# Half of each modulation row handed from VectorE to ScalarE and GpSimd during the SwiGLU stages

## The chip, the cores and the metric

The kernel runs on one core of a Trainium2 chip. The metric is the device time of one execution in microseconds (us). The engines are named as in the profile: PE is TensorE (matmul), PEld its weight load, DVE VectorE, ACT ScalarE, POOL GpSimd, SP SyncE, which here only issues DMAs. A "q" behind an engine's name (SPq, ACTq) means its instruction queue.

## What is computed

A two-layer decoder trunk on 256 tokens of width 1024 in float32. Each layer is a half-step SwiGLU feed-forward (width 2816), a token mixer (block-sparse attention, "MoBA", in the first layer; latent attention, "MLA", in the second), and another half-step SwiGLU. Each of these six sub-layers starts with an RMS norm that is modulated by a shift and a scale, and ends in a gate; all three vectors come from a conditioning vector `c`:

```
mods = silu(c) @ ada_w[layer] + ada_b[layer]          # 1024 x 9216 per layer
sh1, sc1, g1, sh2, sc2, g2, sh3, sc3, g3 = split(mods, 9)
h = rms_norm(x, g) * (1 + sc) + sh
x = x + 0.5 * gate * ((silu(h @ w_gate) * (h @ w_up)) @ w_down)
```

The shared keys and values of MLA have a shift and a scale of their own (`kv_ada_w`, 1024 x 2048). So there are 20 modulation vectors of 1024 numbers. The first two are made at the start in code of their own; the other 18 are what this change is about.

## The kernel before, in words

**Matmuls.** A float32 product is done as three products of split operands (`mm3`, lines 393 to 397): each operand is split into a rounded part `hi` and a rest `lo`. For a weight tile, `split` (lines 174 to 179) lets ACT copy 1024 columns of `raw` into `hi`, and DVE subtract to get `lo = raw - hi`. Hidden activations are split in the same way (`gh`/`gl`, `hh`/`hl`). All of these are recorded under lines 196 and 198, inside the helper `in_turn`, so the profile tells them apart by tile names.

**Loading weights.** `wload` (360 to 380) issues a DMA of up to 1 MB from SP's queue into one of three `raw` buffers and splits it. `hi` and `lo` have eight buffers of 1024 columns each, and `nextw` keeps one load ahead (`LOOK = 1`). A `raw` buffer is free again when DVE has made its `lo`.

**Modulation vectors.** `ada_vec` (201 to 235) makes one vector of 1024 numbers. For each of eight blocks of 128 rows of the weight (`k` from 0 to 7) it loads a 128 x 1024 block into one of three `adaw` buffers from SP's queue (line 209), and DVE adds it, times a column of `silu(c)`, to the 128 x 1024 accumulator `acc` (line 211, one `scalar_tensor_tensor`). I call one such step a row. The bias row is preloaded into the tile `bz`, which stands in for `acc` in the first step. After the eighth row the accumulator is summed over partitions on PE, by transposes and a reduction (lines 222 and 257) for shift and scale, or by a matmul with ones (230 and 231) for gates. There is one `acc` buffer. 

**The order of the work.** Rows are woven into the stages by a clock that adds up estimated PE time (`pe`, `ada_pace`, `ada_until`): in each SwiGLU stage (`ffn`, 506 to 589) they are spread evenly over `FFN_PACE` = 172 us, and what is left is emitted before the next norm (line 584). Stage one gets five vectors (40 rows), MoBA one (8 rows), the second SwiGLU six (48 rows), the third five (40), the last one (8). `tc.issue_after` (in `behind`) keeps rows behind the hand-ordered start-up. Beyond that a scheduler places instructions in the engines' queues; each engine runs its queue strictly in order, and waits on semaphores where an operand or a buffer is not ready.

**The stages in time** (from the trace): start to 47 us; first SwiGLU to about 236; MoBA to about 369; second SwiGLU to about 561; third to about 757; MLA to about 870; last SwiGLU to the end. During the first SwiGLU the kernel also builds MoBA's bias table: DVE makes one-hot tiles `oh`, PE multiplies them, ACT copies them to `bt`, POOL masks two of them (`affine_select`, line 785), and SP writes them to memory (line 788).

**Other lines named below.** POOL raises to a power for every inverse standard deviation: `rstd` (429 for the norms, 992 for MLA's latents) and `hr` (703 for heads). MLA's latent norm is `lat_norm_T` (985 to 1004): ACT squares (`junk`, 988), DVE adds epsilon (`var`, 990), POOL takes the power, DVE scales (`ly`, 994). `head_rstd` (695 to 704) begins with ACT's `sq` (698).

Of the kernel before, what the change touches and what calls it, by code (L numbers as in the profile page):

```python
# [14 lines left out]
AF = mybir.ActivationFunctionType  # L15
ALU = mybir.AluOpType
# [5 lines left out]
D = 1024  # L22
# [65 lines left out]
def trunk(ctx: ExitStack, tc: tile.TileContext, a: dict, out: bass.AP):  # L88
    nc = tc.nc
# [14 lines left out]
    def nm(s):  # L104
        uid[0] += 1
        return f"{s}_{uid[0]}"
# [9 lines left out]
    def later(us, fn):  # L116
        uid[0] += 1
        bisect.insort(pend, (clock[0] + us, uid[0], fn))
# [11 lines left out]
    def pe(us):  # L130
        clock[0] += us
        if busy[0]:
            return
        while pend and pend[0][0] <= clock[0]:
            run_next()
        while pace[0] and clock[0] >= pace[1]:
            pace[1] += pace[0]
            ada(1)
# [15 lines left out]
    bz = cp.tile([P, D], F32, name="bz")  # L154
# [7 lines left out]
    cact = cp.tile([P, KD], F32, name="cact")  # L162
# [11 lines left out]
    def split(src, n):  # L174
        hi = splitp.tile([P, n], F32R, tag="hi", name=nm("hi"))
        lo = splitp.tile([P, n], F32R, tag="lo", name=nm("lo"))
        in_turn(nc.scalar.activation, hi, src, AF.Copy, on="a")
        in_turn(nc.vector.tensor_tensor, lo, src, hi.bitcast(F32), op=ALU.subtract, on="v")
        return hi, lo
# [4 lines left out]
    @contextmanager  # L184
    def behind(*engines):

        with ExitStack() as es:
            for e in engines:
                if e in chain:
                    es.enter_context(tc.issue_after(chain[e].ins))  # L190
            yield

    def in_turn(fn, *args, on="p", **kw):
# [4 lines left out]
            chain[on] = fn(*args, **kw)  # L198
        return chain[on]

    def ada_vec(w, b, col, finish, rows):


        acc = adap.tile([P, D], F32, tag="acc", name=nm("acc"), bufs=1)
        nc.scalar.dma_start(bz[0:1, :], b[col:col + D].rearrange("(o n) -> o n", o=1))
        for k in range(KD):
            wt = adap.tile([P, D], F32, tag="adaw", name=nm("adaw"))
            with behind("s"):
                nc.sync.dma_start(wt, w[k * P:(k + 1) * P, col:col + D])
            with behind("v"):  # L210
                nc.vector.scalar_tensor_tensor(acc, wt, cact[:, k:k + 1], bz if k == 0 else acc,  # L211
                                               op0=ALU.mult, op1=ALU.add)
            if k < KD - 1:
                yield
        if rows:
            ahi, alo = split(acc, D)

        def col_sums():
            for hh in range(2):
                pt = ps_tr.tile([P, 512], F32, tag="tr", name=nm("adaps"))  # L220
                for j in range(4):
                    nc.tensor.transpose(kslice(pt, j), kslice(acc, 4 * hh + j), ident)  # L222
                pe(0.44)
                finish(hh, pt)

        def sums():
            for hh in range(2):
                pt = ps_tr.tile([P, 512], F32, tag="tr", name=nm("adaps"))
                sl = slice(hh * 512, (hh + 1) * 512)
                nc.tensor.matmul(pt, ones_r, ahi[:, sl], start=True, stop=False)  # L230
                nc.tensor.matmul(pt, ones_r, alo[:, sl], start=False, stop=True)
                pe(0.44)
                finish(hh, pt)
        later(3.0, sums if rows else col_sums)
        yield
# [58 lines left out]
    def ada(n):  # L294
        for _ in range(n):
            if next(ada_it, "end") != "end":
                ada_done[0] += 1
# [7 lines left out]
    def ada_until(vectors):  # L305
        pace[0] = None
        while ada_done[0] < vectors * KD:
            ada(1)
# [90 lines left out]
    def mm_tile():  # L399
        return ps_mm.tile([P, 512], F32, tag="mm", name=nm("mm"))  # L400
# [101 lines left out]
    def kslice(tile_, k):  # L502
        return tile_[:, k * P:(k + 1) * P]


    def ffn(layer, idx, h, after, ada_to, start=None):

        last = (layer, idx) == (1, 1)
        with ExitStack() as st:
            gp = st.enter_context(tc.tile_pool(name=nm("gp"), bufs=1))  # L510
            gT = {}
            accs = start() if start else {t: [] for t in range(NT)}
            ada_pace(ada_to, 90.0 if last else FFN_PACE)
            parts = [] if start else [[], []]
            for t in range(NT):
                for i, pl in enumerate(parts):
                    ps = mm_tile()
                    for k in range(KD):
                        if len(pl) <= k:
                            pl += nextw()  # L520
                        mm3(ps, *hk(h[t], k), *pl[k], start=k == 0, stop=k == KD - 1)
                    accs[t].append(ps)
                acc = accs.pop(t)
                g = gp.tile([P, FB], F32, tag="g", name=nm("g"), bufs=2)
                nc.scalar.activation(g, acc[0], AF.Silu)
                nc.vector.tensor_tensor(g, acc[1], g, op=ALU.mult)

                def fin(t=t, g=g):
                    pt = tr_tile()
                    for j in range(FB // P):  # L530
                        nc.tensor.transpose(kslice(pt, j), kslice(g, j), ident)
                    pe(FB // P * 0.11)
                    gh, gl = [gp.tile([P, FB], F32R, tag=f"{nme}_{t}", name=nm(nme)) for nme in ("gh", "gl")]
                    split_evac(gh, gl, pt)
                    for j in range(FB // P):
                        gT[j, t] = (kslice(gh, j), kslice(gl, j))
                later(G_WAIT, fin)
            gq = gp
            for f0 in range(FB, F, S):
                if f0 == SIDE_TO * S:  # L540
                    while start and next(side[0], "end") != "end":
                        bias_step()
                    gq = st.enter_context(tc.tile_pool(name=nm("gp"), bufs=1))
                if start and f0 == ROPE_AT * S:
                    with behind("v", "a", "g"):
                        rope_tables()
                        mla_consts()
                parts = [[], []]
                for f in range(f0 // P, (f0 + S) // P):
                    ps = mm_tile().rearrange("p (i t q) -> p i t q", i=2, q=P)  # L550
                    for i, pl in enumerate(parts):
                        for k in range(KD):
                            if len(pl) <= k:
                                pl += nextw()
                            mm3(ps[:, i], *[w[:, f * P - f0:(f + 1) * P - f0] for w in pl[k]],
                                *hk_both(h, k), start=k == 0, stop=k == KD - 1)
                            if start and k in HOOKS and f0 < SIDE_TO * S:
                                bias_step()
                    g = gp.tile([P, NT, P], F32, tag="gT", name=nm("g"), bufs=2)
                    nc.scalar.activation(g, ps[:, 0], AF.Silu)  # L560
                    nc.vector.tensor_tensor(g, ps[:, 1], g, op=ALU.mult)  # L561
                    gh, gl = [gq.tile([P, NT, P], F32R, tag=f"{nme}{f}", name=nm(nme)) for nme in ("gh", "gl")]
                    split_evac(gh, gl, g)
                    for t in range(NT):
                        gT[f, t] = gh[:, t, :], gl[:, t, :]
            for half in range(2):
                acc = [mm_tile() for _ in range(NT)]
                wl = []

                def mms(t, k):  # L570
                    until(lambda: (k, t) in gT)
                    mm3(acc[t], *gT[k, t], *wl[k], start=k == 0, stop=k == KF - 1)

                lag = LAG if half == 1 else 0
                for k in range(KF):
                    if len(wl) <= k:
                        wl += nextw()
                    mms(0, k)
                    if k - lag >= 0:
                        mms(1, k - lag)  # L580
                gate = mod((layer, 2 * idx), "g")
                resid(0, half, acc[0], gate, last)
                if half == 1:
                    ada_until(ada_to)
                    after(0)
                    for k in range(KF - lag, KF):
                        mms(1, k)
                resid(1, half, acc[1], gate, last)
            after(1)
# [695 lines left out]
```

## Time and profile before

| | |
|---|---|
| median of 3 runs | 1062.43 us (1061.85 to 1064.68) |
| the profiled execution's own time | 1067.16 us |
| its span, first to last instruction | 1065.4 us |
| mean granted clock of TensorE | 0.998 |
| PE busy in the span | 1020.8 us (96%) |
| ACT busy | 578.6 us (54%) |
| data moved by DMA | 260.65 MB, mean 245 GB/s |

The profile gives, for one execution, the busy time of each engine, groups of instructions by line and shape, what each wait ended on, and a timeline. "Busy" of PE is drawn from modelled ends of pipelined matmuls, so gaps of a fraction of a microsecond inside a dense run do not show. In the tables by stretch, the figure behind an engine is its busy time inside that stretch, with the number of instructions in brackets.

### The profile page before, as it was taken

How to read it: one execution, taken by the hardware profiler on the slowest of the kernel's cores; microseconds unless marked ns; L12 is line 12 of the kernel's file. 1: busy time of each engine (PE TensorE's matmuls, PEld its weight loads, DVE VectorE, ACT ScalarE, POOL GpSimd, SP SyncE). 2: the span in 40 equal slices, each digit the busy share in tenths (PEclk: the TensorE clock that was granted, in tenths of full speed). 3: DMA queues.
4: the chain of work that ended last, by engine and by line, in shares of the span. 5: the costliest groups of instructions: out<-in, count | busy, mean ns of one | idle time of the engine just before them, and what ended most of it. 6: DMA issues, size and time to landing. Idle time of an engine off the chain costs nothing.

```text
span 1065.4 us, 17278 instructions
## 1 busy us (share of the span) xinstructions
PE 1020.8 (96%) x6663; PEld 899.3 (84%) x6663; DVE 810.9 (76%) x1244; ACT 578.6 (54%) x1048; POOL 70.1 (7%) x119
## 2 busy tenths in 40 slices
PE   4999999998999999999999999999988899999998
PEld 2499999886778789999887999988766778999986
DVE  5999977886875789889688888867778758755642
ACT  4364545357675765545348544533868777545531
POOL 4001000002121000000000000000043200000000
PEclk9999999999999999999999999999999999999999
DMA  9999987996845479989897997986354337665450
GB/s 311 322 304 287 376 288 278 335 318 206 310 162 170 139 236 345 337 293 332 295 313 227 328 329 251 318 303 205 117 162 142 119 119 236 223 204 187 161 177 20
DMA packets 166934, 260.65 MB, mean 245 GB/s; under 512 B 8030, under 2 KB 110214, under 8 KB 166852
## 3 DMA queue, kind: packets, MB, share of 16 engines
q1 hardware_dynamic: 164496, 254.70, 70.3%
q0 software_dynamic: 976, 3.37, 1.0%
q10 hardware_dynamic: 1380, 1.49, 0.5%
q8 instruction: 52, 0.85, 0.3%
q14 instruction: 30, 0.25, 0.1%
HBM read 255.33 MB, written 4.19 MB: 244 GB/s over the span
## 4 chain that ended last, share of the span: by engine, by line
PE 77%; DVE 10%; ACT 4%; DMA 4%; POOL 3%; issue 3%; SPq 0%; DVEq 0%; ACTq 0%; POOLq 0%
PE mm L394 23%; PE mm L396 23%; PE mm L395 23%; DVE lo L196 3%; POOL hr L703 3%; DMA adaw<-in_ada_w_dram 2%; PE mm L198 2%; ACT hi L196 1%; DVE oh L722 1%; PE adaps L222 1%; PE at L666 1%; PE at L611 1%; DVE acc L211 1%; DMA raw<-in_ffn_w_gate_dram 1%; ACT y L196 1%
## 5 line engine op out<-in xcount | busy, mean ns | idle before, releaser
L196 DVE TENSOR_TENSOR lo<-raw,hi 128x1024 fp32r<-128x1024 f32 (+2 forms) x316 | 374.3, 1199 | 80.2 <-ACT hi L196 79.3
L196 ACT ACTIVATE hi<-raw 128x1024 fp32r<-128x1024 f32 (+2 forms) x316 | 324.1, 1040 | 171.5 <-PE mm L396 103.6
L394 PE MATMUL mm<-hh,hi 128*128 128x256 f32 x1152 | 328.6, 285 | 0.0
L396 PE MATMUL mm<-hh,lo 128*128 128x256 f32 x1152 | 326.7, 284 | 0.5 <-DVE lo L196 0.5
L395 PE MATMUL mm<-hl,hi 128*128 128x256 f32 x1152 | 326.5, 283 | 0.0
L395 PEld LDWEIGHTS mm<-hl,hi 128*128 128x128 f32 x1152 | 221.7, 192 | 0.6 <-issue 0.2
L396 PEld LDWEIGHTS mm<-hh,lo 128*128 128x128 f32 x1152 | 221.6, 192 | 0.7 <-DVE lo L196 0.7
L394 PEld LDWEIGHTS mm<-hh,hi 128*128 128x128 f32 x1152 | 221.7, 192 | 0.6 <-issue 0.2
L211 DVE SCALAR_TENSOR_TENSOR acc<-adaw,cact,acc 128x1024 f32<-128x1024 f32 x126 | 162.8, 1292 | 20.6 <-DMA adaw<-in_ada_w_dram 16.2
L394 PE MATMUL mm<-hi,gh 128*128 128x512 f32 x352 | 138.0, 392 | 0.0
L395 PE MATMUL mm<-lo,gh 128*128 128x512 f32 x352 | 137.0, 389 | 0.0
L396 PE MATMUL mm<-hi,gl 128*128 128x512 f32 x352 | 137.0, 389 | 0.0
L394 PE MATMUL mm<-hi,hh 128*128 128x512 f32 (+1 forms) x240 | 96.7, 404 | 5.0 <-ACT hh L196 5.0
L396 PE MATMUL mm<-hi,hl 128*128 128x512 f32 (+1 forms) x240 | 94.0, 392 | 1.5 <-DVE hl L196 1.4
L395 PE MATMUL mm<-lo,hh 128*128 128x512 f32 (+1 forms) x240 | 93.4, 390 | 0.0
L560 ACT ACTIVATE g<-mm 128x256 f32<-128x256 f32 x72 | 27.3, 379 | 94.5 <-PE mm L396 94.5
L396 PEld LDWEIGHTS mm<-hi,gl 128*128 128x128 f32 x352 | 66.1, 188 | 13.8
L394 PEld LDWEIGHTS mm<-hi,gh 128*128 128x128 f32 x352 | 66.1, 188 | 13.2
L395 PEld LDWEIGHTS mm<-lo,gh 128*128 128x128 f32 x352 | 66.1, 188 | 13.1
L196 ACT ACTIVATE gh<-g 128x256 fp32r<-128x256 f32 x72 | 29.9, 416 | 69.6 <-DVE g L561 69.6
L394 PEld LDWEIGHTS mm<-hi,hh 128*128 128x128 f32 x240 | 45.1, 188 | 16.1 <-ACT hh L196 7.8
L396 PEld LDWEIGHTS mm<-hi,hl 128*128 128x128 f32 x240 | 45.1, 188 | 13.2 <-DVE hl L196 4.5
(222 smaller groups left out, 1114.8 us busy)
## 6 DMA issues: line engine op xcount, KB each, us to landing
adaw<-in_ada_w_dram SPq DMA_DIRECT2D x144, 512.0 KB, 6.8
raw<-in_ffn_w_gate_dram SPq DMA_DIRECT2D x42, 1024.0 KB, 7.3
raw<-in_ffn_w_up_dram SPq DMA_DIRECT2D x42, 1024.0 KB, 6.9
raw<-in_ffn_w_down_dram SPq DMA_DIRECT2D x40, 1024.0 KB, 6.6
raw<-in_moba_w_qkv_dram SPq DMA_DIRECT2D x16, 512.0 KB, 5.0
adaw<-in_kv_ada_w_dram SPq DMA_DIRECT2D x16, 512.0 KB, 5.6
raw<-in_ffn_w_down_dram SPq DMA_DIRECT2D x8, 512.0 KB, 3.6
raw<-in_moba_w_qkv_dram SPq DMA_DIRECT2D x4, 1024.0 KB
```

What stands on the lines that cost most here:

```text
L196: return fn(*args, **kw)
L198: chain[on] = fn(*args, **kw)
L211: nc.vector.scalar_tensor_tensor(acc, wt, cact[:, k:k + 1], bz if k == 0 else acc, op0=ALU.mult, op1=ALU.add)
L222: nc.tensor.transpose(kslice(pt, j), kslice(acc, 4 * hh + j), ident)
L394: nc.tensor.matmul(ps, lh, rh, start=start, stop=False)
L395: nc.tensor.matmul(ps, lh, rl, start=False, stop=False)
L396: nc.tensor.matmul(ps, ll, rh, start=False, stop=stop)
L560: nc.scalar.activation(g, ps[:, 0], AF.Silu)
L611: nc.tensor.matmul(ps3[:, i, :], qTs(e, t), kTs(e, nk), start=bias is not None, stop=bias is not None or i == len(es) - 1)
L666: nc.tensor.matmul(po[i * DH:(i + 1) * DH, pr, t, :], vs(e, kb), pT[t, e, kb], start=kb == 0, stop=kb == t)
L703: nc.gpsimd.tensor_tensor(r, v2, mhalf[:, :nh], op=ALU.pow)
L722: return fn(*args, **kw)
```

## The change

In the SwiGLU stages DVE does only the left 512 columns of each row (`acc[:, :n]`). For the right 512 columns ACT multiplies the loaded block by the column of `silu(c)` in place, and POOL adds it to the accumulator. A flag, set when a SwiGLU stage is entered and cleared just before the next norm, says where this holds: 136 of the 144 rows; the eight rows of the MoBA stage stay whole on DVE.

```diff
+    shared = [False]
+
     def ada_vec(w, b, col, finish, rows):
...
             with behind("s"):
                 nc.sync.dma_start(wt, w[k * P:(k + 1) * P, col:col + D])
+            old = bz if k == 0 else acc
+            n = D // 2 if shared[0] else D
             with behind("v"):
-                nc.vector.scalar_tensor_tensor(acc, wt, cact[:, k:k + 1], bz if k == 0 else acc,
+                nc.vector.scalar_tensor_tensor(acc[:, :n], wt[:, :n], cact[:, k:k + 1], old[:, :n],
                                                op0=ALU.mult, op1=ALU.add)
+            if n < D:
+                with behind("a", "g"):
+                    nc.scalar.activation(wt[:, n:], wt[:, n:], AF.Copy, scale=cact[:, k:k + 1])
+                    nc.gpsimd.tensor_tensor(acc[:, n:], wt[:, n:], old[:, n:], op=ALU.add)
             if k < KD - 1:
                 yield
...
     def ffn(layer, idx, h, after, ada_to, start=None):
 
         last = (layer, idx) == (1, 1)
+        shared[0] = True
...
                 if half == 1:
                     ada_until(ada_to)
+                    shared[0] = False
                     after(0)
```

How the queues move: PE's order is the same but for one exchange of two neighbours. ACT's queue gains 136 multiplications and POOL's 136 additions. An `adaw` buffer is now free for the next load when both DVE and POOL have read it. In the bias phase of the first SwiGLU POOL's first `affine_select` stands behind the first seven additions, and one weight tile ("up") whose load SP issued ahead of eight writes of the bias table is now issued behind them. At the start of MLA three additions of the last vector stand among the `rstd` of line 992, two ahead of the third and one ahead of the fourth, and the third multiplication stands in ACT's queue ahead of the fourth `junk` of line 988.

## The prediction

> **What bounds the kernel now.** I read the page's first part, then the busy time of each engine by stretch, then the rows of line 211 in the same stretches.
>
> ```profile
> PE 1020.8 (96%) x6663; PEld 899.3 (84%) x6663; DVE 810.9 (76%) x1244; ACT 578.6 (54%) x1048; POOL 70.1 (7%) x119
> ```
>
> ```profile
> core 0: us, PE busy (x) PEld busy (x) DVE busy (x) ACT busy (x) POOL busy (x), PEclk, DMA share, GB/s
> 47.00:91.00 44.00, 41.97 (x487) 36.13 (x486) 42.41 (x96) 24.86 (x60) 2.06 (x1) 1.00 0.84 270
> 91.00:200.00 109.00, 109.00 (x817) 104.47 (x818) 95.87 (x141) 54.35 (x89) 3.23 (x1) 0.98 0.92 321
> 200.00:248.00 48.00, 46.21 (x212) 37.36 (x211) 36.77 (x41) 26.90 (x48) 2.79 (x5) 1.00 0.89 314
> 370.00:520.00 150.00, 150.00 (x1085) 141.75 (x1084) 128.71 (x145) 81.27 (x122) 0.56 (x1) 1.00 0.89 307
> 520.00:757.00 237.00, 235.67 (x1486) 213.07 (x1484) 189.32 (x219) 117.80 (x179) 1.65 (x3) 1.00 0.81 275
> 757.00:870.00 113.00, 101.45 (x616) 82.33 (x615) 87.59 (x207) 82.31 (x207) 26.98 (x22) 1.00 0.41 132
> ```
>
> PE is the bound: 96% of the span, and in the SwiGLU stages (the first five stretches) it is idle for 44.00 - 41.97 = 2.0, 0, 1.8, 0 and 1.3 us, 5.1 us in all. That is all that a freer DVE could win there, less what is hidden in modelled matmul ends. DVE is second: 96% busy in 47 to 91, 88% in 91 to 200, 86% in 370 to 520, 80% in 520 to 757. POOL is nearly unused. The same stretches for line 211 alone (DVE busy and count):
>
> ```profile
> 47.00:91.00 44.00, 7.64 (x6) 1.00 0.84 270
> 91.00:200.00 109.00, 33.67 (x25) 0.98 0.92 321
> 200.00:248.00 48.00, 11.53 (x9) 1.00 0.89 314
> 370.00:520.00 150.00, 49.85 (x39) 1.00 0.89 307
> 520.00:757.00 237.00, 61.34 (x48) 1.00 0.81 275
> ```
>
> **What the change takes from DVE.** Lengths: the whole row from the rows of line 211, a quarter row from the same operation at the start, ACT's and POOL's nearest rows of 512 columns.
>
> ```profile
> L211 DVE SCALAR_TENSOR_TENSOR acc<-adaw,cact,acc x126: 1254/1277/3023, 65.1 to 914.9; 128x1024 f32<-128x1024 f32 x126
> ```
>
> ```profile
> L198 DVE SCALAR_TENSOR_TENSOR acc<-adaw,cact,acc 128x256 f32<-128x256 f32 x56 | 23.0, 478 | 0.4 <-DMA adaw<-in_ada_w_dram 0.3
> ```
>
> ```profile
> L196 ACT ACTIVATE junk<-x 128x512 bf16<-128x512 f32 x20 | 12.6, 630 | 19.3 <-DVE x L496 19.3
> ```
>
> ```profile
> L971 POOL TENSOR_SCALAR_AFFINE_SELECT mask<-mask 128x512 bf16<-128x512 bf16 x2 | 1.2, 622 | 0.0
> ```
>
> 1277 ns for 1024 columns and 478 for 256 make (1277 - 478) / 768 = 1.04 ns a column, so half a row takes 478 + 256 x 1.04 = 744 ns. DVE saves 0.53 us a row, 136 x 0.53 = 72 us in all. ACT gains 136 x 0.63 = 86 us. It lies beside PE: ACT is at 50 to 56% in the long SwiGLU stretches and stays under 75%; without that cover it would cost 0.63 us a row. So far nothing is lost, and at most 5 us are to be won.
>
> **What POOL's additions cost DVE.** No two-input addition of this size is in the trace. But twice POOL worked over a large tile while DVE was busy:
>
> ```profile
> 77.99 2.06 POOL L785 TENSOR_SCALAR_AFFINE_SELECT bt<-bt 128x2048 f32<-128x2048 f32 x1 [55.97 <-ACT bt L722]
> 95.04 3.23 POOL L785 TENSOR_SCALAR_AFFINE_SELECT bt<-bt 128x2048 f32<-128x2048 f32 x1 [14.99 <-DMA adaw<-in_ada_w_dram]
> ```
>
> ```profile
> 77.61 3.49 DVE L722 TENSOR_SCALAR oh<-posq,key 128x128 bf16<-128x128 f32 x8
> ```
>
> ```profile
> 84.49 1.64 DVE L722 TENSOR_SCALAR oh<-posq,key 128x128 bf16<-128x128 f32 x8
> ```
>
> ```profile
> 95.18 1.22 DVE L196 TENSOR_TENSOR lo<-raw,hi 128x1024 fp32r<-128x1024 f32 x1
> 96.32 3.02 DVE L211 SCALAR_TENSOR_TENSOR acc<-adaw,cact,acc 128x1024 f32<-128x1024 f32 x1
> ```
>
> Alone the mask takes 2.06 us. The second came while DVE made a `lo` (until 96.40) and took 3.23, 1.17 more: it waited for that `lo`. Then DVE's row, started at 96.32, took 3.02 instead of 1.28, 1.74 more: it waited for POOL until about 98.1, where POOL ended at 98.27. Beside the first mask eight one-hot compares took 3.49 instead of 1.64, 1.85 more. So in this trace the two engines take turns, for whole instructions, and each loses nearly all of the other's time.
>
> An addition's own length I bound by POOL's rows: not less than the 0.62 us of a one-input pass over 512 columns, not more than the 2.06 us of one over 2048. The two passes give (2.06 - 0.62) / 1536 = 0.94 ns a column and 0.14 us fixed; two inputs read one after the other would take 0.14 + 2 x 512 x 0.94 / 1000 = 1.10 us. I take 1.10, nearer the lower row. Each row then costs DVE 1.10 - 0.53 = 0.57 us more than before, with ends of +0.09 and +1.53. By stretch, DVE's new demand against the room:
>
> - 47 to 200: 42.41 + 95.87 + 31 x 0.57 = 155.9 of 153, over by 2.9.
> - 200 to 248: 36.77 + 9 x 0.57 = 41.9 of 48, room.
> - 370 to 520: 128.71 + 39 x 0.57 = 150.9 of 150, over by 0.9.
> - 520 to 757: 189.32 + 48 x 0.57 = 216.7 of 237, room.
>
> The last SwiGLU has eight rows and much room. A queue in order is never quite full: of the 14.7 and 21.3 us that DVE is idle today in the two tight stretches (153 - 138.3; 150 - 128.7), mostly in front of an ACT result, I leave a seventh, 2.1 and 3.0 us. PE then waits for `lo` by 2.9 + 2.1 = **5.0 us** in the first SwiGLU and 0.9 + 3.0 = **3.9 us** in the second, **0** in the others. PE's idle time of today stays, since in 47 to 91 it is DVE that PE waits for.
>
> [...]
>
> **What the new waits cost in the queues.** Two places stand out in the new order. First, the bias phase:
>
> ```profile
> 82.30 0.37 SPq L370 DMA_DIRECT2D raw<-in_ffn_w_up_dram  x1
> 82.72 7.72 SPq L788 DMA_DIRECT2D bias_d<-bt  x8
> ```
>
> This "up" tile goes behind the eight bias writes, which themselves wait for the mask, now behind seven additions. So it leaves not at 82.3 but at 91 to 100, and lands some 6 us later. ACT splits it at 100.3 today, and PE reaches it at about 112 by the count of matmuls before it (an estimate). That is just covered; if not, the cost is up to 5 us. I take **1.0 us**.
>
> Second, the start of MLA, where each latent norm is on the chain that ends last:
>
> ```profile
> L209 SPq DMA_DIRECT2D adaw<-in_ada_w_dram x128: 327/328/1552, 41.5 to 907.8; - x128
> ...
> DMA to landing us min/median/max: 3.5/6.3/7.7
> ```
>
> ```profile
> 772.24 0.33 SPq L209 DMA_DIRECT2D adaw<-in_ada_w_dram  x1
> ```
>
> ```profile
> 776.25 0.38 ACT L988 ACTIVATE junk<-mm 128x256 bf16<-128x256 f32 x1 [0.36 <-PE mm L396]
> ```
>
> ```profile
> 777.93 1.39 POOL L992 TENSOR_TENSOR rstd<-var,mhalf 128x1 f32<-128x1 f32 x1 [0.72 <-DVE var L990]
> ```
>
> The third block of the last vector is asked for at 772.24 and lands at 772.24 + 6.3 = 778.5 (775.7 to 779.9). ACT's third multiplication waits for it, and behind it in ACT's queue wait the fourth `junk` (776.25 today), both `kpe` and the first `sq`; POOL's addition then stands ahead of the fourth `rstd` (777.93 today). Multiplication until 779.2, addition until 780.3: the `rstd` comes at 780.3, **2.4 us** later, and PE, idle for 11.5 us in this stage already, has nothing to fill the gap. Ends: 0 (landing in 3.5 us) to 3.8.
>
> [...]
>
> **The sum.** 5.0 + 3.9 + 1.0 + 2.4 = 12.3 us. The profiled execution itself would go from 1067.16 to 1079.5; it stands 4.7 above the median of the runs, so on the median 1062.43 + 12.3 = 1074.7 us.
>
> **Rivals.**
>
> 1. *Cheap additions.* If an addition holds DVE for about 0.62 us, DVE's demand rises by 0.09 us a row and fits everywhere. The queue terms stay, 0 to 4 us, and up to 2 of the 5.1 us of PE idle come back: 1061 to 1066, about 1064. For it: POOL's fixed pass of 0.62. Against: it has two operands to read.
>
> 2. *Faster.* The additions fall mostly beside DVE's own waits or beside instructions that do not take turns with POOL. The point from which this decides is 0.53 us of blocked DVE time a row: below it DVE is freer than today. Then the 2.0 us in 47 to 91, where DVE sets PE's pace, the 1.8 and 1.3 after it and gaps hidden in modelled ends go, at no loss at MLA if the block lands early: 1062.43 - 5 = 1057. For it: DVE is 96% busy where PE waits. Against: the three collisions above, each at full price.
>
> 3. *Dear additions.* At 1.40 us the excess is 0.87 us a row. The tight stretches are over by 12.3 (138.28 + 31 x 0.87 = 165.3 against 153) and 12.6 (128.71 + 39 x 0.87 = 162.6 against 150), with the same leftovers and queue terms 12.3 + 12.6 + 5.1 + 3.4 = 33.4, or 1096. At 2.06 (+1.53) the stretches are over by 33 (47 to 200), 3, 38 and 26, about 1165.
>
> **How the numbers follow.** The forecast (slower by 4 to 22 us) gets 0.52. Cheap additions get 0.17, of which 0.04 end over 0.3% slower. Faster gets 0.15. Dear additions get 0.16, of which 0.08 lie above 1094. Three tenths of a per cent, 3.2 us, is about what a measurement of this kernel can tell from no change. Faster by more: 0.15; within: 0.13; slower: 0.52 + 0.04 + 0.16 = 0.72. The range from 1059 to 1094 leaves out about 0.10 below and 0.08 above; the forecast's own range is 1066 to 1084.
>
> **What would show it.** In the profile of the changed kernel: line 211's half rows near 744 ns where POOL is idle and well over a microsecond where it is not; `lo` of 128 x 1024 with a mean above 1220 ns, for the same reason; POOL's additions with a shortest near 1.10 us; DVE near 100% in 91 to 200 and 370 to 520; PE waiting for DVE's `lo` there; PE busy time unchanged, with 12 us more idle. At MLA the fourth `rstd` of line 992 comes about 2.4 us later after the third, behind an addition. The prediction is wrong if `lo` keeps 1220 ns beside additions (rival 2), if the shortest addition is near 0.6 (rival 1) or over 1.4 (rival 3), or if the loss sits in stages whose demand I found to fit.

## The result, and the profile of the changed kernel

The changed kernel takes 1103.9 us (median of 4 runs, 1102.3 to 1109.1) against 1063.4 us (4 runs, 1061.9 to 1064.7): a ratio of 1.039, 95% interval 1.0351 to 1.0429. The forecast was 1074.7 us, with a range up to 1094: the direction was right, the loss three times too small.

Its profiled execution has a span of 1103.1 us at a mean granted clock of 0.988. First the busy times, from the page:

```profile
PE 1035.0 (94%) x6663; PEld 905.9 (82%) x6663; DVE 850.8 (77%) x1244; ACT 654.2 (59%) x1183; POOL 303.1 (27%) x254
```

The span grew by 37.7 us. PE is idle for 1103.1 - 1035.0 = 68.1 us in place of 44.6, 23.5 more, and the other 14.2 us are longer busy time of PE for the same matmuls, most of it at a lower clock (last section). DVE, whose part of each row the change halves, is busy for 39.9 us *more*. The same stretches of time as before (the work in them has shifted by up to 35 us):

```profile
47.00:91.00 44.00, 40.33 (x445) 33.78 (x444) 44.00 (x86) 26.91 (x64) 18.93 (x9) 1.00 0.76 251
91.00:200.00 109.00, 107.68 (x833) 103.89 (x832) 96.13 (x144) 63.81 (x108) 36.64 (x22) 0.97 0.88 300
370.00:520.00 150.00, 142.92 (x1042) 134.72 (x1042) 129.79 (x139) 92.55 (x156) 56.74 (x35) 0.99 0.78 262
520.00:757.00 237.00, 226.62 (x1407) 203.53 (x1407) 191.51 (x202) 143.17 (x217) 82.37 (x49) 0.97 0.83 281
```

DVE is full in the first only; in 91 to 200 it is at 88% and in 370 to 520 at 87%, and yet PE loses time. Where it goes by stage is read from the first `rstd` of each sub-layer in the timeline of POOL (line 429 before, 438 after). For the second SwiGLU, before and then after (start, length):

```profile
364.56 0.56 POOL L429 TENSOR_TENSOR rstd<-var,mhalf 128x1 f32<-128x1 f32 x1 [24.32 <-DVE var L427]
557.77 0.55 POOL L429 TENSOR_TENSOR rstd<-var,mhalf 128x1 f32<-128x1 f32 x1 [187.16 <-DVE var L427]
```

```profile
376.22 0.56 POOL L438 TENSOR_TENSOR rstd<-var,mhalf 128x1 f32<-128x1 f32 x1 [3.67 <-DVE var L436]
586.61 0.55 POOL L438 TENSOR_TENSOR rstd<-var,mhalf 128x1 f32<-128x1 f32 x1 [9.63 <-DVE var L436]
```

That is 193.21 us before and 210.39 after. In the same way:

| stage | forecast | measured |
|---|---|---|
| first SwiGLU | 6.0 | 10.9 |
| MoBA | 0 | 0.8 |
| second SwiGLU | 3.9 | 17.2 |
| third SwiGLU | 0 | 6.5 |
| MLA | 2.4 | 2.0 |
| last SwiGLU | 0 | 0.4 |

The groups of instructions by shape (busy, mean ns | idle before them), three of them before and then after:

```profile
L196 DVE TENSOR_TENSOR lo<-raw,hi 128x1024 fp32r<-128x1024 f32 x300 | 361.5, 1220 | 75.5 <-ACT hi L196 74.7
L196 DVE TENSOR_TENSOR gl<-g,gh 128x256 fp32r<-128x256 f32 x72 | 30.3, 420 | 14.4 <-ACT gh L196 14.3
L561 DVE TENSOR_TENSOR g<-mm,g 128x256 f32<-128x256 f32 x72 | 30.1, 418 | 30.8 <-ACT g L560 30.8
```

```profile
L196 DVE TENSOR_TENSOR lo<-raw,hi 128x1024 fp32r<-128x1024 f32 x300 | 401.9, 1360 | 80.8 <-ACT hi L196 80.6
L221 POOL TENSOR_TENSOR acc<-adaw,acc 128x512 f32<-128x512 f32 x119 | 208.2, 1750 | 252.4 <-ACT adaw L220 221.9 <-PE at L657 14.3 <-issue 8.4
L216 DVE SCALAR_TENSOR_TENSOR acc<-adaw,cact,acc 128x512 f32<-128x512 f32 x119 | 129.9, 1092 | 14.4 <-DMA adaw<-in_ada_w_dram 9.5 <-DMA adaw<-in_kv_ada_w_dram 3.8
L196 DVE TENSOR_TENSOR gl<-g,gh 128x256 fp32r<-128x256 f32 x72 | 41.0, 569 | 19.9 <-ACT gh L196 19.9
L571 DVE TENSOR_TENSOR g<-mm,g 128x256 f32<-128x256 f32 x72 | 29.9, 415 | 24.6 <-ACT g L570 24.6
```

DVE's half row takes 1092 ns on average, POOL's addition 1750, and `lo`, which has nothing to do with the rows, 140 ns more than before. The shortest ones say what they take alone:

```profile
L216 DVE SCALAR_TENSOR_TENSOR acc<-adaw,cact,acc x126: 734/752/1799, 64.2 to 952.6; 128x512 f32<-128x512 f32 x119, 128x1024 f32<-128x1024 f32 x7
L221 POOL TENSOR_TENSOR acc<-adaw,acc x119: 1256/1630/4037, 52.9 to 950.2; 128x512 f32<-128x512 f32 x119
```

0.73 us for the half row (forecast 0.744) and 1.26 us for the addition (forecast 1.10). All else is waiting. A stretch of the timeline shows it, DVE first and then POOL:

```profile
531.54 1.78 DVE L216 SCALAR_TENSOR_TENSOR acc<-adaw,cact,acc 128x512 f32<-128x512 f32 x1
533.24 2.31 DVE L196 TENSOR_TENSOR lo<-raw,hi 128x1024 fp32r<-128x1024 f32 x1
535.47 1.77 DVE L216 SCALAR_TENSOR_TENSOR acc<-adaw,cact,acc 128x512 f32<-128x512 f32 x1
537.17 1.21 DVE L196 TENSOR_TENSOR lo<-raw,hi 128x1024 fp32r<-128x1024 f32 x1
```

```profile
530.26 6.43 POOL L221 TENSOR_TENSOR acc<-adaw,acc 128x512 f32<-128x512 f32 x3 [6.47 <-ACT adaw L220]
```

Three rows are added back to back: POOL needs 6.43 us for 3 x 1.26 = 3.8 us of work, and three of DVE's instructions in a row (1.78, 2.31, 1.77) take 1.04 to 1.09 us more than alone (0.73, 1.22, 0.73). In this stretch the two engines alternate, instruction by instruction.

### The profile page after: what moved, and what is told of

Its sections match the earlier page's. It is cut to its first block, busy times and chain, and to the rows that moved or that the text cites. A ratio compares the mean times of both kernels' runs of the same rounds, so it can differ in the third digit from the quotient of the medians.

```text
span 1103.1 us, 17838 instructions
## 1 busy us (share of the span) xinstructions
PE 1035.0 (94%) x6663; PEld 905.9 (82%) x6663; DVE 850.8 (77%) x1244; ACT 654.2 (59%) x1183; POOL 303.1 (27%) x254
## 4 chain that ended last, share of the span: by engine, by line
PE 54%; DVE 20%; DMA 9%; issue 7%; ACT 6%; POOL 4%; SPq 0%; DVEq 0%; ACTq 0%; POOLq 0%
PE mm L403 16%; PE mm L405 16%; PE mm L404 16%; DVE lo L196 8%; DMA adaw<-in_ada_w_dram 5%; DVE acc L216 3%; POOL hr L714 3%; ACT hi L196 3%; DMA adaw<-in_kv_ada_w_dram 2%; PE mm L198 2%; DVE oh L733 1%; PE at L677 1%; ACT y L196 1%; PE at L622 1%; DMA raw<-in_ffn_w_down_dram 1%
## 5 line engine op out<-in xcount | busy, mean ns | idle before, releaser
L196 DVE TENSOR_TENSOR lo<-raw,hi 128x1024 fp32r<-128x1024 f32 (+2 forms) x316 | 415.2, 1333 | 84.0 <-ACT hi L196 83.7
L196 ACT ACTIVATE hi<-raw 128x1024 fp32r<-128x1024 f32 (+2 forms) x316 | 319.6, 1036 | 87.8 <-PE mm L405 39.7
L221 POOL TENSOR_TENSOR acc<-adaw,acc 128x512 f32<-128x512 f32 x119 | 208.2, 1750 | 252.4 <-ACT adaw L220 221.9
L216 DVE SCALAR_TENSOR_TENSOR acc<-adaw,cact,acc 128x512 f32<-128x512 f32 (+1 forms) x126 | 138.9, 1102 | 16.0 <-DMA adaw<-in_ada_w_dram 11.1
L220 ACT ACTIVATE adaw<-adaw,cact 128x512 f32<-128x512 f32 x135 | 96.6, 719 | 91.7 <-DMA adaw<-in_ada_w_dram 61.7
L221 POOL TENSOR_TENSOR acc<-adaw,bz 128x512 f32<-128x512 f32 x16 | 25.0, 1560 | 167.4 <-PE adaps L231 56.8
```

The source lines that it names most:

```text
L196: return fn(*args, **kw)
L216: nc.vector.scalar_tensor_tensor(acc[:, :n], wt[:, :n], cact[:, k:k + 1], old[:, :n], op0=ALU.mult, op1=ALU.add)
L220: nc.scalar.activation(wt[:, n:], wt[:, n:], AF.Copy, scale=cact[:, k:k + 1])
L221: nc.gpsimd.tensor_tensor(acc[:, n:], wt[:, n:], old[:, n:], op=ALU.add)
```

## The experiments

A ratio is always against the kernel before, run on the same chip in the same rounds. Three theories stood at the start. **T1**: the turns that VectorE and GpSimd take cost the time. **T2**: ScalarE's multiplication stands at the head of its queue until the row has landed, and the `hi` splits wait behind it (ACT's multiplications wait 81.8 us for landings in the changed kernel). **T3**: the row buffers come free later, so that rows and weights are asked for later.

**Which of the three engines' parts costs the time.** Without the multiplication:

```diff
-                    nc.scalar.activation(wt[:, n:], wt[:, n:], AF.Copy, scale=cact[:, k:k + 1])
```

> The changed kernel without ScalarE's multiplication: GpSimd adds the unmultiplied right half (so the scaling of these columns is left out). VectorE and GpSimd still take turns, and GpSimd still holds each row's buffer. Theory T1 (the turns of VectorE and GpSimd cost the time): nearly all of the 40 us stay, 1095 to 1104. Theory T2 (the multiplication waits for its row's landing at the head of ScalarE's queue, and the hi splits wait behind it): most of it goes, 1066 to 1080. Theory T3 (the buffers come free later, so rows and weights are asked for later): most stays, since the addition still ends last, 1090 to 1104.

With an addition of 8 columns:

```diff
-                    nc.gpsimd.tensor_tensor(acc[:, n:], wt[:, n:], old[:, n:], op=ALU.add)
+                    nc.gpsimd.tensor_tensor(acc[:, n:n + 8], wt[:, n:n + 8], old[:, n:n + 8], op=ALU.add)
+                    if k == 0:
+                        nc.gpsimd.memset(acc[:, n + 8:], 0.0)
```

> The changed kernel with its multiplication, but GpSimd adds only 8 of the 512 columns (the other columns of the right half are left out, set to zero once per vector). GpSimd's passes become short, so the turns nearly go; the wait of ScalarE for the landing stays, and the buffer comes free some 1.2 us earlier than in the changed kernel. T1: VectorE is freer than in the kernel before, 1058 to 1066. T2: 1085 to 1100. T3: in between, 1070 to 1090.

With VectorE's half alone:

```diff
-                    nc.scalar.activation(wt[:, n:], wt[:, n:], AF.Copy, scale=cact[:, k:k + 1])
-                    nc.gpsimd.tensor_tensor(acc[:, n:], wt[:, n:], old[:, n:], op=ALU.add)
+                    if k == 0:
+                        nc.gpsimd.memset(acc[:, n:], 0.0)
```

> The changed kernel with neither the multiplication nor the addition: VectorE does the left half of each row and the right half is left out (set to zero once per vector). It shows what the saving of 0.53 us a row on VectorE is worth by itself. The prediction has at most 5 us to be won: 1057 to 1064 under every theory. Over 1066 would say that the saving itself disturbs the order; under 1055 that VectorE was more of a bound than its waits showed.

With the addition on VectorE:

```diff
-                    nc.gpsimd.tensor_tensor(acc[:, n:], wt[:, n:], old[:, n:], op=ALU.add)
+                    nc.vector.tensor_tensor(acc[:, n:], wt[:, n:], old[:, n:], op=ALU.add)
```

> The changed kernel with the right half's addition on VectorE in place of GpSimd; ScalarE still multiplies, everything is computed. No turns to take, but VectorE waits for ScalarE's multiplication in each row and works some 0.2 us a row more than in the kernel before. T1: 1064 to 1075 (136 x 0.2 = 27 us more on VectorE, which mostly fits). T2: 1090 to 1110, since ScalarE still waits for landings, and now VectorE waits for ScalarE besides. T3: 1065 to 1085.

| run | us | ratio, 95% interval | DVE busy |
|---|---|---|---|
| no multiplication | 1101.3 | 1.0339, 1.0292 to 1.0385 | 861.4 |
| addition of 8 columns | 1066.8 | 1.0017, 0.9998 to 1.0036 | 746.6 |
| VectorE's half alone | 1068.4 | 1.0027, 1.0008 to 1.0046 | 746.1 |
| addition on VectorE | 1074.7 | 1.0095, 1.0067 to 1.0122 | 819.1 |

T2 falls: without the multiplication nearly all of the loss stays, and with it, but without a long addition, all of it goes. The multiplication may cost some 5 us beside the turns (1.039 against 1.0339), but the intervals overlap. The addition on VectorE loses 10 us without turns, though VectorE is only 8 us busier and waits for the multiplication for 0.6 us; where that loss comes from stays open. The line of the half alone is worth a look:

```profile
PE 1022.6 (96%) x6663; PEld 902.1 (85%) x6663; DVE 746.1 (70%) x1244; ACT 580.1 (54%) x1048; POOL 80.0 (7%) x135
```

VectorE has 64.8 us less to do than before, and the kernel is not faster. There was nothing to be won; at 0.3% over the kernel before it even came out above what had been expected (1057 to 1064), so the new order may cost a little by itself. The same line gives the price of a turn: 850.8 - 746.1 = 104.7 us over the 135 rows that show in the trace, on average 0.78 us a row in which VectorE counts as busy and waits for GpSimd.

**Buffers, length and stage.** The next run keeps the length of GpSimd's work, but lets the row's buffer go:

```diff
-                    nc.scalar.activation(wt[:, n:], wt[:, n:], AF.Copy, scale=cact[:, k:k + 1])
-                    nc.gpsimd.tensor_tensor(acc[:, n:], wt[:, n:], old[:, n:], op=ALU.add)
+                    nc.gpsimd.tensor_tensor(acc[:, n:n + 8], wt[:, n:n + 8], old[:, n:n + 8], op=ALU.add)
+                    nc.gpsimd.tensor_tensor(acc[:, n:], bz[:, n:], old[:, n:], op=ALU.add)
```

> As the changed kernel without ScalarE's multiplication, but GpSimd's long addition no longer reads the row: an addition of 8 columns waits for the row and lets its buffer go, and behind it the addition of 512 columns runs over the running sum and the bias tile, which stay in place (the right half's weights are left out but for 8 columns). GpSimd takes as long per row as before, VectorE still keeps its left half, and the buffer comes free over 1.2 us earlier. T1 (turns of VectorE and GpSimd): 1095 to 1110, as much as the changed kernel loses or a little more. T3 (buffers held by GpSimd, so that rows and weights are asked for later): 1064 to 1075.

Three others change one size each: `n = 3 * D // 4` (a quarter shared), `n = D // 4` (three quarters), and the stage:

```diff
-        shared[0] = True
+        shared[0] = (layer, idx) == (1, 0)
```

> The changed kernel with 256 of the 1024 columns on ScalarE and GpSimd in place of 512; everything is computed. By T1 the addition of 256 columns holds the port for some 0.65 us (half of 1.26 and a fixed part), VectorE saves 256 x 1.04 = 0.27 us, so the row costs 0.38 us where the half row costs 1.26 - 0.53 = 0.73: about half of the changed kernel's loss, 1076 to 1090. If the loss came from the number of passes or hand-overs and not from their length, it would stay at 1095 to 1104.

> The changed kernel, but rows are shared in the third SwiGLU stage alone (520 to 757 us of the kernel before; 48 of the 136 rows); everything is computed. The prediction found room there, 216.7 us of VectorE's time against 237, and a cost of 0: 1062 to 1066. If the 6.4 us that the changed kernel loses there are the stage's own and not carried over from the stage ahead: 1068 to 1073, MLA's 2 us among them.

> The changed kernel with 768 of the 1024 columns on ScalarE and GpSimd; everything is computed. By T1 the addition holds the port for some 1.87 us and VectorE saves 0.80 us, so the row costs 1.07 us where the half row costs 0.73: with a loss of 40 us for the half row about 59 us, more if waits pile up, 1115 to 1150. If VectorE's own work were what counts (the saving of 0.80 us a row), it would be below the changed kernel, under 1100.

| run | us | ratio, 95% interval | DVE busy |
|---|---|---|---|
| buffer let go | 1094.5 | 1.0264, 1.0232 to 1.0296 | 847.8 |
| a quarter shared | 1074.8 | 1.0093, 1.0058 to 1.0128 | 822.0 |
| third SwiGLU alone | 1069.7 | 1.0039, 1.0022 to 1.0055 | 821.2 |
| three quarters shared | 1143.4 | 1.0727, 1.0697 to 1.0757 | 877.0 |

T3 falls as the main cause: without the multiplication SP waited for POOL's additions for only 4.5 us in all, and the loss was 36 us; with the buffers let go it waited 1.6 us, and the loss is still 29. The second run is not a clean test by itself: the long addition reads the bias tile, and ScalarE's queue, which issues the bias loads, waits 65.8 us for it. What the 7 us between the two come from stays open. The length of the addition sets the loss, and more than in proportion: 10, 41 and 77 us for 256, 512 and 768 columns. With the third SwiGLU alone (40 rows, the five vectors of that stage) the stage takes 755.45 - 558.93 = 196.5 us against 193.1, so 3.4 of the 6.5 us are its own; the other half comes only when the stages ahead are shared too. MLA takes 872.30 - 755.45 = 116.9 us there against 117.3 before: with the last vector's rows whole, MLA's 2 us are gone.

```profile
558.93 0.55 POOL L438 TENSOR_TENSOR rstd<-var,mhalf 128x1 f32<-128x1 f32 x1 [189.77 <-DVE var L436]
755.45 0.55 POOL L438 TENSOR_TENSOR rstd<-var,mhalf 128x1 f32<-128x1 f32 x1 [9.94 <-DVE var L436]
872.30 0.56 POOL L438 TENSOR_TENSOR rstd<-var,mhalf 128x1 f32<-128x1 f32 x1 [24.43 <-DVE var L436]
```

**More row buffers.** The idea was a ring: VectorE late, buffer late, transfer late, VectorE without data. Memory for two more row buffers came from one pair of split buffers, which needs a control:

```diff
-    splitp = ctx.enter_context(tc.tile_pool(name="splitp", bufs=8))
-    adap = ctx.enter_context(tc.tile_pool(name="adap", bufs=3))
+    splitp = ctx.enter_context(tc.tile_pool(name="splitp", bufs=7))
+    adap = ctx.enter_context(tc.tile_pool(name="adap", bufs=5))
```

> The changed kernel with 7 buffers each for hi and lo in place of 8 and the row buffers left at 3: the control of the next run, which needs that memory. Fewer split buffers mean that splits are made less far ahead of the matmuls: as the changed kernel, 1100 to 1104, to 1112 if the depth of the split buffers is what carries VectorE's delays.

> The changed kernel with 5 row buffers in place of 3 and 7 hi and lo buffers in place of 8. VectorE and GpSimd take turns as before, but SyncE's queue, in which weight tiles stand behind rows, no longer waits for the row that was added last. If late buffers pass the turns on as late landings (the ring: VectorE late, buffer late, transfer asked for late, VectorE and TensorE without data): 1075 to 1090, 15 us or more below the control. If the turns cost time as plain work of VectorE: within 4 us of the control.

> The kernel before with 5 row buffers in place of 3 and 7 hi and lo buffers in place of 8. TensorE is its bound with 5 us of waits in the SwiGLU stages, so neither the buffers taken nor those given can win much: 1060 to 1067 under every theory; above 1070 would say that the eighth pair of split buffers carried something.

The control took 1119.7 us (1.0510, 1.0490 to 1.0529), the changed kernel with 5 rows 1131.8 (1.0625, 1.0607 to 1.0643), the kernel before with 5 rows 1070.0 (1.0044, 1.0029 to 1.0059). The ring gets no support: SP did wait less for rows (the longest waits of its queue, control and then 5 rows), and the kernel got slower.

```profile
SPq L379 <- DVE lo L196: 499.5, 120, 22.5
SPq L212 <- DVE acc L216: 203.1, 92, 8.5
```

```profile
SPq L379 <- DVE lo L196: 573.3, 128, 22.5
SPq L212 <- DVE acc L216: 132.0, 61, 10.4
```

But one pair of split buffers less costs the changed kernel 1.2%, some 13 us, where buffers and rows together cost the kernel before 0.4%. The split buffers are the cushion between DVE and PE, and with turns the kernel seems to live off it; the next paragraph has another reason.

In these kernels the scheduler had also moved the rows in DVE's queue. Averaged over the 208 instructions that add to `acc`, one has 0.39 fewer `lo` of weights ahead of it in the changed kernel than in the kernel before, 0.81 in the control and 1.24 with 5 rows. (64 of the 208 are the quarter rows of the start, which stay where they are; over the 144 rows it is 0.56, 1.17 and 1.79.) Hence **T4**: the rows stand ahead of `lo` splits that TensorE needs. The test issues each row's arithmetic with the next row's transfer (shown), or the one after that:

```diff
             with behind("s"):
                 nc.sync.dma_start(wts[k], w[k * P:(k + 1) * P, col:col + D])
+            if k:
+                add(k - 1)
             if k < KD - 1:
                 yield
+        add(KD - 1)
```

Here `add(k)` holds the instructions of row k, which stood behind the transfer.

> The changed kernel, but each row's arithmetic (all three engines' part) is issued when the next row's transfer is, one step later; everything is computed. In VectorE's queue the rows then stand 0.21 weight splits (lo) earlier than in the kernel before, on average; in the changed kernel 0.39 earlier. Theory T4 (the order that was built puts rows ahead of lo splits that TensorE needs, and the turns make each such place dear): some 15 us below the changed kernel, 1083 to 1094. T1 alone (the turns cost time wherever they fall): within 5 us of the changed kernel, 1099 to 1109. T3 (buffers held longer cost time): above it, over 1109.

> As the run before, but two steps later; the rows then stand on average where the kernel before has them (0.01 lo splits earlier), and all three row buffers are in use. T4: below the run with one step, 1068 to 1085. T1 alone: 1099 to 1109. T3: over 1109.

> The control: the kernel before, unshared, with each row's arithmetic two steps later (0.45 lo splits later on average). Without turns to take the place of a row should matter little: 1060 to 1067 by T1 and T4; over 1070 by T3, since the buffers are held two steps longer.

They took 1099.9 us (1.0324, 1.0299 to 1.0349), 1100.8 (1.0323, 1.0295 to 1.0351) and 1066.6 (1.0007, 0.9991 to 1.0023). One step wins about 0.7%, the second nothing more: T4 is a small part.

**Plain time against turns.** So the turns cost the time, but is it because VectorE has more to do (**T5**), or because of what a turn is (**T6**)? The first two runs give VectorE more work without GpSimd, each row in 2 or 4 instructions:

```diff
-                nc.vector.scalar_tensor_tensor(acc, wt, cact[:, k:k + 1], bz if k == 0 else acc,
+                for c in range(0, D, D // 4):
+                    s = slice(c, c + D // 4)
+                    nc.vector.scalar_tensor_tensor(acc[:, s], wt[:, s], cact[:, k:k + 1], (bz if k == 0 else acc)[:, s],
```

> The kernel before, but each row on VectorE in two instructions of 512 columns; ScalarE and GpSimd do nothing of it, everything is computed. Two halves take 2 x 0.744 = 1.49 us where a row takes 1.28: 144 x 0.21 = 30 us more on VectorE, without turns. If VectorE's time is what counts although it is idle for a seventh of the stage (theory T5: in effect it is the bound as soon as it gets slower), about as much is lost: 1085 to 1098. If only the collisions count, in which a lo split that TensorE needs waits for GpSimd: 1063 to 1072.

> The same with four instructions of 256 columns: 4 x 0.478 = 1.91 us a row, 144 x 0.63 = 91 us more on VectorE, still without turns. T5: 1130 to 1160. If only collisions count: up to what the room leaves, by the sums of the prediction 47 to 200: 42.4 + 95.9 + 31 x 0.63 = 157.8 of 153, 370 to 520: 128.7 + 39 x 0.63 = 153.3 of 150, so 8 to 25 us, 1073 to 1090.

The other two add turns to the kernel before, whose order of rows and splits stays (0.01 `lo` earlier):

```diff
+            if shared[0]:
+                with behind("g"):
+                    nc.gpsimd.tensor_tensor(spare[:, :8], wt[:, :8], bz[:, :8], op=ALU.add)
+                    nc.gpsimd.tensor_tensor(bz[:, :W], bz[:, :W], bz[:, :W], op=ALU.subtract)
```

> The kernel before with VectorE's whole rows and its own order of rows and lo splits; beside each of the 135 rows GpSimd, once the row has landed, subtracts 512 columns of the bias tile from themselves, work that nobody needs (the bias has been used by then; everything is computed). Only the turns are added. From the changed kernel VectorE's instructions should grow by some 0.78 us a row ((850.8 - 746.1) / 135), 105 us in all, about as much plain time as the four quarters gave (91 us, loss 11). If VectorE's time is what counts, wherever it comes from: 1076 to 1090. If turns are dearer than the same time planned into the order (theory T6: they come in bunches when rows land, and fall on the lo splits that TensorE needs next): 1115 to 1165.

> The control of the run before: GpSimd's passes have 8 columns in place of 512, all else is the same. 1063 to 1069 under every theory; more would say that the waits on the bias tile, and not the turns, cost the time.

| run | us | ratio, 95% interval | DVE busy |
|---|---|---|---|
| rows in two halves | 1069.1 | 1.0038, 1.0016 to 1.0061 | 827.2 |
| rows in four quarters | 1077.1 | 1.0104, 1.0071 to 1.0138 | 861.1 |
| turns alone, 512 columns | 1117.2 | 1.0488, 1.0468 to 1.0508 | 897.7 |
| the same with 8 columns | 1074.8 | 1.0088, 1.0071 to 1.0104 | 810.8 |

The pieces followed each other more tightly than expected: VectorE got 16 and 50 us more, not 30 and 91. T5 falls: those 50 us cost 11, while the changed kernel's 40 us cost 38 of span.

The sharpest comparison needs no further run. Four quarters and the changed kernel without its multiplication have the same busy time of VectorE (861.1 and 861.4 us), one by planned work and one by turns. The second SwiGLU, from its first `rstd` to the next one, in the kernel before, in four quarters and then without the multiplication:

```profile
364.56:557.77 193.21, 191.08 (x1269) 175.14 (x1269) 162.14 (x181) 101.00 (x154) 1.11 (x3) 1.00 0.87 300
```

```profile
370.06:566.60 196.54, 193.73 (x1283) 177.14 (x1282) 178.17 (x322) 99.57 (x154) 1.11 (x2) 1.00 0.86 293
```

```profile
374.30:583.14 208.84, 199.72 (x1282) 181.42 (x1282) 178.13 (x181) 97.02 (x154) 76.70 (x46) 0.97 0.81 277
```

VectorE is busy for 178.2 us in both, 16 more than before; as planned work that costs the stage 3.3 us, through turns 15.6. The order of the rows is not the reason: with the order of the kernel before (two steps later, above) the loss stayed at 3.2%. What differs is where the time falls: planned work is an instruction of its own, which the order was built around; a turn lengthens an instruction that stands there (in the changed kernel `lo` from 1220 to 1360 ns on average).

The turns alone cost 51 us, of which the control, itself 9 us above the expected zero, leaves 42. This pair is less clean: GpSimd also writes the bias tile, and ScalarE's `hi`, `gh` and `g` wait for that, 35.1 us in the control and 64.1 in the turns alone, so a part of the 42 may be these waits. Turns come in runs, as in this stretch of the turns alone, DVE and then PE:

```profile
575.05 1.73 DVE L196 TENSOR_TENSOR lo<-raw,hi 128x1024 fp32r<-128x1024 f32 x1
577.31 3.38 DVE L215 SCALAR_TENSOR_TENSOR acc<-adaw,cact,acc 128x1024 f32<-128x1024 f32 x2
580.61 2.06 DVE L196 TENSOR_TENSOR lo<-raw,hi 128x1024 fp32r<-128x1024 f32 x1
```

```profile
582.73 0.50 PE L403 MATMUL mm<-lo,gh 128*128 128x512 f32 x1 [2.87 <-DVE lo L196]
```

A `lo`, two rows and the next `lo` take 0.5, 0.8 and 0.8 us more than alone (1.22, 2 x 1.27, 1.22), and PE waits 2.87 us for the last of them. That turns cost more than the same time as split rows is shown; that it is because they come in runs on the `lo` splits is read from these timelines and was not tried by itself. Nor is all planned work cheap: the addition on VectorE cost 10 us for 8, without turns.

**What stays open.** Per microsecond that DVE grew by, four quarters cost 0.2 us, the turns alone (51 - 9) / 87 = 0.5, the run without the multiplication 36 / 50 = 0.7, the one with the buffers let go 29 / 37 = 0.8 and the changed kernel about 1. The order of the rows (up to 0.7%) and the multiplication (up to 0.5%) would make up much of the difference between the last ones, but their intervals are too wide to say so. Nothing tried points to a version that beats the kernel before: with the other half of the work left out altogether, it is not faster.

## Why the prediction was wrong

- **What bounds the kernel, and what could be won: right.** PE is the bound; VectorE's half alone wins nothing (at most 5 us had been said).
- **The half row: right.** 734 ns against 744. ACT's pass took 719 ns on average (630), and its cover held: with the multiplication and a short addition the ratio is 1.0017.
- **The addition: too short.** 1.26 us in place of 1.10. By the prediction's own sum with 1.26 - 0.53 = 0.73 us a row, the tight stretches are over by 138.28 + 31 x 0.73 - 153 = 7.9 and 128.71 + 39 x 0.73 - 150 = 7.2 us, and with the leftovers (2.1 and 3.0) and the queue terms (1.0 and 2.4) 23.6 us are lost: 1086. That is 11 of the missing 29 us. The measured time lies in the span that rival 3 (dear additions) gave, 1096 and up, but not for its reason: its addition takes 1.40 us or more.
- **The turns: right in kind.** They are whole instructions, and they also hit `lo` (1220 to 1360 ns, as said). In the stretch shown a collision costs "nearly all of the other's time", as said (1.04 to 1.09 us of 1.26), but on average a row costs 0.78 us, less than the 1.10 that the sum charged. The expectations for a quarter and for three quarters say that the addition "holds the port": no run shows a port, and what the runs showed in its place is longer instructions of VectorE, 1092 ns on average for a half row whose shortest took 734.
- **The sum by stretch: the step that failed.** "DVE's new demand against the room" took a stage for an account in which DVE's idle time pays for turns. With the measured growth of 40 us over 135 rows, 0.30 a row, both tight stretches would have fitted (138.28 + 9.2 = 147.5 of 153; 128.71 + 11.5 = 140.2 of 150), even with the 2.1 and 3.0 us left over, so PE would have had nothing to wait for, and the sum would be the 3.4 us of the queue terms. In its place the runs showed that VectorE's idle time did not absorb the turns: in the second SwiGLU the same 16 us more of VectorE cost 15.6 us as turns and 3.3 as planned work. The sign "DVE near 100% in 91 to 200 and 370 to 520" did not come (88% and 87%), while PE waited there and even in 520 to 757, where there was room (the last sign of being wrong that the prediction named). The account nearly held for the split rows (50 us more, 11 lost); it did not for the turns (40 us more, 38 lost).
- **The third SwiGLU at 0:** the stage by itself loses 3.4 us though its account had room, and the other half appears only with the stages ahead shared too, which the prediction had not thought of.
- **"PE busy time unchanged": wrong.** It grew by 14.2 us, some 10 of it through the clock; see the last section.
- **The "up" tile: the move is right**, the cost unseen: it left at 94.45, between 91 and 100 as said.

```profile
94.45 0.85 SPq L379 DMA_DIRECT2D raw<-in_ffn_w_up_dram  x1
```

- **MLA: the number near (2.0 us for 2.4), the mechanism mostly not.** The last vector's shared rows are the cause: with them whole, the loss is gone. But the third multiplication did not wait for its block's landing; it follows `qlT` without a gap. The `rstd` of line 1003 (992 before), the additions, DVE's instructions that changed and ACT's third multiplication, before and then after:

```profile
772.42 1.21 POOL L992 TENSOR_TENSOR rstd<-var,mhalf 128x1 f32<-128x1 f32 x2 [11.90 <-DVE var L990]
776.65 0.55 POOL L992 TENSOR_TENSOR rstd<-var,mhalf 128x1 f32<-128x1 f32 x1 [3.03 <-DVE var L990]
773.68 0.41 DVE L196 TENSOR_TENSOR hkv<-z,hkv 128x256 fp32r<-128x256 f32 x1
774.54 0.95 DVE L196 TENSOR_TENSOR lo<-raw,hi 128x768 fp32r<-128x768 f32 x1
```

```profile
807.50 1.27 POOL L1003 TENSOR_TENSOR rstd<-var,mhalf 128x1 f32<-128x1 f32 x2 [11.90 <-DVE var L1001]
813.32 0.55 POOL L1003 TENSOR_TENSOR rstd<-var,mhalf 128x1 f32<-128x1 f32 x1 [1.89 <-DVE var L1001]
813.83 1.29 POOL L221 TENSOR_TENSOR acc<-adaw,acc 128x512 f32<-128x512 f32 x1
815.08 1.53 POOL L1003 TENSOR_TENSOR rstd<-var,mhalf 128x1 f32<-128x1 f32 x1
808.82 1.48 DVE L196 TENSOR_TENSOR hkv<-z,hkv 128x256 fp32r<-128x256 f32 x1
810.75 1.49 DVE L196 TENSOR_TENSOR lo<-raw,hi 128x768 fp32r<-128x768 f32 x1
811.86 0.71 ACT L220 ACTIVATE adaw<-adaw,cact 128x512 f32<-128x512 f32 x1
```

From the first to the fourth `rstd` it was 777.93 - 772.42 = 5.5 us and is 7.6, 2.1 more. Of these, 1.6 are there already at the third (4.2 and then 5.8 us): two of DVE's instructions ahead of its `var` take turns with the first two additions and grow by 1.07 and 0.54 us. Only the last 0.5 us is the fourth `rstd` behind the third addition. That the sum came out near is luck.

- **One sum comes out a little differently.** The stretches of rival 3 at 2.06 us, with the leftovers and queue terms, add up to about 1171, not 1165. That does not change the forecast.
- **Row buffers that come free later: not the main cause, but not shown to be free.** The sum charges nothing for them. SP's wait for POOL's additions came to 44.6 us in the changed kernel. With 5 row buffers it fell to 1.5 us (42.4 in the control), and the kernel got slower; but the order had changed as well.

## What to carry to other kernels

Work that went from VectorE to GpSimd was not taken off VectorE here: every 1.26 us on GpSimd held VectorE for 0.78 us, more than the 0.53 us that were saved. Before giving work to another engine, run the kernel with that work left out: here that won nothing, which settles the matter in one run. An account of busy time against room by stage came near for the split rows here, which the order was built around (0.2 us for each microsecond that VectorE grew by); the waits that arose at run time cost 0.5 to 1 us for each.

## What the runs showed of the hardware

**After a gap PE ran at half clock for a time.** In the changed kernel PE waits for one `hi`, and then runs slowly:

```profile
565.82 0.39 PE L405 MATMUL mm<-hi,gl 128*128 128x512 f32 x1
569.90 0.79 PE L403 MATMUL mm<-hi,gh 128*128 128x512 f32 x1 [3.69 <-ACT hi L196]
571.45 0.80 PE L404 MATMUL mm<-lo,gh 128*128 128x512 f32 x1 [0.75 <-DVE lo L196]
```

```profile
570.00:574.00 4.00, 3.25 (x7) 2.28 (x8) 3.14 (x3) 2.03 (x3) 1.19 (x2) 0.50 0.91 366
574.00:578.00 4.00, 4.00 (x15) 3.20 (x15) 4.00 (x4) 2.72 (x4) 2.90 (x2) 0.79 0.42 109
578.00:588.00 10.00, 8.87 (x46) 7.13 (x44) 7.07 (x9) 6.17 (x9) 1.39 (x2) 1.00 1.01 381
```

Some 2.6 us into the 3.69 us without work the granted clock falls to 0.50 (it is 1.00 from 568.0 to 568.5 and 0.50 from 569.0 on), and it stays there until about 575.6; matmuls of 512 columns then start every 0.43 us where they start every 0.23 us before the gap and from 576 on. The ten that start from 571.45 to 575.45 take 4.33 us in place of 2.3: on top of the gap of 3.69 us that is 2.0 us more. Between the start and the last microseconds the changed kernel has six such stretches of half clock, 23.9 us in all, and the kernel before one of 3.4 us; that makes the mean clock 0.988 in place of 0.998. The 20.5 us more at half clock account for some 10 of PE's 14.2 us; what the other 4 come from is not shown. In the turns alone half clock follows a shorter wait, the one of 2.87 us above that ends at 582.73.

```profile
584.00:587.00 3.00, 3.00 (x8) 2.30 (x7) 3.00 (x2) 0.00 (x0) 1.87 (x3) 0.50 0.72 227
```

**Which of VectorE's instructions take turns.** `g<-mm,g`, with one operand in PSUM (the matmul's result) and one in SBUF, kept its 418 ns (415 after), and `gl<-g,gh` of the same 256 columns, with both in SBUF, went from 420 to 569. Of the 72 `g`, 19 fall beside an addition of GpSimd and take 414 ns on average; of the 72 `gl`, 15 do and take 1014. The two differ, among other things, in where one operand lies; that this makes the difference was not tried by itself.
